# Inverse softmax sums turned by TensorE transposes instead of a trip through DRAM, with new delays for the instruction streams

## The chip, the core and the metric

The kernel runs on one core of a Trainium2 chip. A core has a matrix engine (TensorE, PE in the profile), a vector engine (VectorE, DVE), an engine for activation functions and copies (ScalarE, ACT), a general engine (GpSimd, POOL) and a queue that issues most of the transfers (SyncE, SP). Each takes its instructions in the order in which they were written for it, and waits on semaphores for the others. TensorE reads SBUF and writes PSUM, which has eight banks of 128 x 512 float32. The metric is the device time of one execution in microseconds (us); lower is better.

## What is computed

One decoder layer on 512 tokens of width 1024, in float32. One projection of the normed input feeds eight heads of block attention (512 columns each for q, k, v) and eight heads of a gated delta rule (`gdn`, chunks of 64 tokens, with a triangular solve per chunk and a scan over the chunks). Both outputs go through one output projection, then comes an MLP with squared ReLU. With two blocks of 256 tokens and up to three selected, the attention here comes down to causal attention with a relative bias:

```python
h = rms_norm(x, pre_mix_norm[l])
proj = jnp.einsum('bsd,dc->bsc', h, w_in[l])
...
o_att = moba_attention(q, k, v, rel_bias)      # softmax(q k / 8 + bias[distance]) v
o_gdn = gated_deltanet(gdn_qkv, gdn_z, gdn_a, gdn_b, conv_w[l], A_log[l], dt_bias[l], gdn_norm_w[l])
mix = jnp.einsum('bsc,cd->bsd', jnp.concatenate([o_att, o_gdn], axis=-1), w_out[l])
x = x + rms_norm(mix, post_mix_norm[l])
h = rms_norm(x, pre_mlp_norm[l])
m = jnp.einsum('bsf,fd->bsd', jnp.square(jax.nn.relu(jnp.einsum('bsd,df->bsf', h, w_up[l]))), w_down[l])
x = x + rms_norm(m, post_mlp_norm[l])
```

The change touches the division by the sum of the softmax, which the kernel does as a product with the inverse sum after P V.

## The kernel before

**Stages.** First the input is scaled and the first four columns of the projection are built (`head`). Then the other columns of the projection run (`projections`, `by_token`), and beside them the attention and the preparation of the delta rule. Every product that must be exact is split: a float32 operand is cut in a high and a low part of a faster format, and three matmuls (`mm3`) stand for one. The attention goes by four pairs of heads, p = 0 to 3. `scores` makes, for a pair, four rows of blocks (q = 3, 2, 1, 0, of 512, 384, 256 and 128 keys): six matmuls from `pt` into PSUM tag `a`, the bias and the row minimum on DVE (L688), and the exponential with its row sum on ACT (L690). Then DVE inverts the sums (L693). `values` turns the blocks of P by TensorE transposes (k = 3 to 0, helper line L103), copies them to SBUF tiles `ph` on ACT (L718), multiplies them by V and, on DVE, multiplies the product by the inverse sums (L738).

**The way of the sums before.** The sums lie with the query on the partition (128 x 4 x 2), but the product P V has the query along the free axis. So the inverse sums are written to DRAM (`d_s`, L694, 1024 single floats) and read back twice, each time spread over 64 partitions (L697), into `R8`. All three transfers are issued by SP, and the two reads wait for the write.

**What sets the order.** PE's order is written out by hand: a small planner (`Weave`) runs the streams (`scores`, `values`, `chunks`, `inverse`, `scan`, `finish_o`, `projections` and others) against a clock of its own that only counts matmul time. A stream gives a delay (`WAIT`, for the n-th use `SINGLE`) or a mark on which it waits, and the one of lowest `RANK` that is due goes next. The other engines' instructions are placed by a scheduler, with `LEAD` as extra urgency for a stream.

**The stages that the prediction speaks of.** `inverse` solves the triangles on DVE, `scan` starts by merging the halves (PE products of 32 x 32, `UT` and `uap` read back from DRAM by L774 and L771), then multiplies `UT` by `kB`, then makes eight steps: PE, a copy `vn` on ACT (L854), PE, DVE. `finish_o` norms the scan's output, and four transposes (`ot`) and the gate `zs` give `mg`. The projection's weights come through two buffers `w_raw` (SP L151), are cut by ACT into `w_hi` (L156) and by DVE or POOL into `w_lo` (L157). The weights of the output projection (`wo_raw`, L143, ACT L144, DVE L145) use the same two buffers at first. After the scan, the rest of the projection's columns and the last pair, PE has only the output projection to do, which starts with `ps_mm<-wo_h,mg_h`. From there to the end one product follows the other.

Of the kernel before, what the change touches and what calls it, by code (L numbers as in the profile page):

```python
# [11 lines left out]
FT = mybir.dt.float32  # L12
# [75 lines left out]
def layer(ctx, tc, nc, x, x_t, x_t0, w_first, w_in, w_v, w_ab, w_out, w_up, w_down, conv_w, a_log, dt_bias, gdn_norm_w, rel_bias,  # L88
# [13 lines left out]
    def transpose(o, i, k=128):  # L102
        nc.tensor.transpose(o, i, ident[:k, :k])  # L103
        weave.now += k * 4 / 2400
# [9 lines left out]
    dram = pool("dram", space=DRAM)  # L114
# [5 lines left out]
    at = pool("att", 2, stack=sA)  # L120
# [56 lines left out]
    def bank(tag="g", shape=(128, 512)):  # L177
        return psum.tile(list(shape), FT, name="ps_" + tag, tag=tag, bufs={"mm": 2, "g": 3, "a": 3}[tag])
# [281 lines left out]
    rkb, egc, gc, gl = (by5[:, i] for i in (1, 3, 4, 5))  # L460
# [198 lines left out]
    rows_of, sums_of = {}, {}  # L659


    def scores():
        for p in range(4):
            yield f"a{p}"
            if p:
                yield f"turned{p - 1}"
            T = [pts[p][:, i] for i in range(4)]
            Es = []
            for hh in range(2):
                E = at.tile([128, 512], FT, name="E")  # L670
                nc.sync.dma_start(E, bass.AP(tensor=d_e.tensor, offset=d_e.offset + 640 * (2 * p + hh), ap=[[1, 128], [1, 512]]))
                Es.append(E)
            Ls = [at.tile([128, 1280], FT, name="L") for _ in range(2)]
            mins = at.tile([128, 4, 2], FT, name="mins")
            sums = at.tile([128, 4, 2], FT, name="sums")
            for q in (3, 2, 1, 0):
                w = 128 * q + 128
                qs = slice(128 * q, 128 * q + 128)
                s = [bank("a") for _ in range(2)]
                for n, (i, j) in enumerate(((0, 2), (0, 3), (1, 2))):  # L680
                    for hh in range(2):
                        hs = slice(64 * hh, 64 * hh + 64)
                        mm(s[hh][:, :w], T[i][hs, qs], T[j][hs, :w], start=n == 0, stop=n == 2)
                weave.now -= 3 * w / 2400
                for hh in range(2):
                    l = Ls[hh][:, 64 * q * (q + 1):64 * q * (q + 1) + w]
                    rows_of[p, hh, q] = l
                    nc.vector.tensor_tensor_reduce(out=l, in0=s[hh][:, :w], in1=Es[hh][:, w - 1::-1], scale=1.0, scalar=3e38,  # L688
                                                   op0=OP.add, op1=OP.min, accum_out=mins[:, q, hh:hh + 1])
# [4 lines left out]
            nc.sync.dma_start(d_s[p].rearrange("q h t -> t q h"), sums)  # L694
            sums_of[p] = at.tile([128, 512], FT, name="R8", bufs=1)
            for hh in range(2):
                nc.sync.dma_start(sums_of[p][64 * hh:64 * hh + 64].rearrange("p (q t) -> p q t", q=4), d_s[p, :, hh].partition_broadcast(64))  # L697
# [4 lines left out]
    def values():  # L702
        for p in range(4):
# [319 lines left out]
    up = lambda g, k: w_up[2 * g:2 * g + 2, k // 4, :, k % 4].rearrange("a p n -> p a n")  # L1023
# [212 lines left out]
    t1, t2 = both[:, :, Z[0]], both[:, :, Z[1]]  # L1236
# [104 lines left out]
    rs = {}  # L1341
# [171 lines left out]
```

## Time and profile before

| what | value |
|---|---|
| median of 3 runs | 659.45 us (654.26 to 661.19) |
| the profiled execution | 654.6 us, its span 652.8 us |
| VectorE, ScalarE, GpSimd busy | 463.9, 354.7, 139.9 us |
| mean clock granted to TensorE | 0.969 |
| bytes moved by DMA | 114.53 MB |

The span is the time from the first to the last instruction of the profiled execution. A line of the timeline gives the start, the duration of the group, engine, line, operation, what it writes and reads, how many instructions, and in brackets how long the engine had been idle and what released it. Matmuls overlap, so the next row's start says more than a row's duration. A line of windows gives a stretch, its length, the busy time of the five engines with the number of instructions, the clock granted to TensorE (1.00 is full), the share of the DMA engines and GB/s.

### The profile page before, as it was taken

Reading aid. Unit: us, or ns where it says so; the run is one execution under the profiler, and the core shown is the slowest. Engines: PE = TensorE matmul, PEld = TensorE weight load, DVE = VectorE, ACT = ScalarE, POOL = GpSimd, SP = SyncE. Lnnn points to the kernel's source line nnn. Section 1 sums busy time; section 2 is a strip of 40 time slices with the busy share of each in tenths; the row PEclk is TensorE's granted clock in tenths of the full one; section 3 lists DMA queues with packets and bytes.
Section 4 is the critical chain, followed back from the end, with each engine's and each line's share of the span. In section 5 each row is a group of like instructions: output and inputs, shape, how many; then the busy total and the mean of one; then the engine's idle time right before and its main releaser. Section 6 shows DMA issues by size and latency. Waiting matters only on the chain.

```text
span 652.8 us, 10879 instructions
## 1 busy us (share of the span) xinstructions
PE 623.8 (96%) x4225; PEld 527.2 (81%) x4225; DVE 463.9 (71%) x673; ACT 354.7 (54%) x598; POOL 139.9 (21%) x176
## 2 busy tenths in 40 slices
PE   9989999999979989499999999999999999999995
PEld 7767777878747778378899899999998888888884
DVE  6688773999505455276564678888779888888876
ACT  8378573353726436244441576566566656655661
POOL 1435636101112232101412112211111230000001
PEclk9999999999959979789999999999999999999999
DMA  9332324323831203393378989999989999967603
GB/s 315 97 91 65 103 77 119 97 77 92 176 43 43 57 33 84 67 306 110 130 265 259 219 217 256 221 257 285 256 234 345 328 293 290 281 193 293 217 1 129
DMA packets 67635, 114.53 MB, mean 175 GB/s; under 512 B 20088, under 2 KB 41720, under 8 KB 67200
## 3 DMA queue, kind: packets, MB, share of 16 engines
q1 hardware_dynamic: 49888, 84.48, 39.7%
q0 software_dynamic: 17696, 29.36, 21.6%
q8 instruction: 33, 0.54, 0.4%
q14 instruction: 18, 0.15, 0.1%
HBM read 108.02 MB, written 35.17 MB: 219 GB/s over the span
## 4 chain that ended last, share of the span: by engine, by line
PE 83%; DMA 7%; DVE 5%; ACT 2%; issue 2%; SPq 1%; POOL 1%; POOLq 0%; DVEq 0%; ACTq 0%
PE ps_mm L99 38%; PE ps_g L99 26%; PE ps_a L99 16%; DMA d_s<-sums 3%; DMA w_raw<-in_w_in 1%; DMA wo_raw<-in_w_out 1%; PE ps_a L103 1%; DVE conv L383 1%; PE ps_g L103 1%; DMA UT<-d_u 1%; ACT w_hi L156 0%; SPq L774 0%; POOL w_lo L157 0%; SPq L697 0%; DVE pt L133 0%
## 5 line engine op out<-in xcount | busy, mean ns | idle before, releaser
L132 ACT CAST wdh<-wd 128x1024 fp32r<-128x1024 f32 x53 | 55.9, 1054 | 51.4 <-PE ps_mm L99 22.6
L133 DVE TENSOR_TENSOR u_l<-w,u_h 128x1024 fp32r<-128x1024 f32 x46 | 56.2, 1224 | 37.2 <-ACT u_h L132 35.5
L133 DVE TENSOR_TENSOR wdl<-wd,wdh 128x1024 fp32r<-128x1024 f32 x53 | 64.9, 1224 | 22.2 <-ACT wdh L132 22.1
L132 ACT CAST u_h<-w 128x1024 fp32r<-128x1024 f32 x46 | 47.9, 1046 | 56.7 <-PE ps_a L99 20.3
L99 PE MATMUL ps_mm<-hT_h,w_hi 128*128 128x512 f32 x168 | 71.1, 423 | 0.0
L99 PE MATMUL ps_mm<-hT_h,w_lo 128*128 128x512 f32 x168 | 66.3, 395 | 0.0
L99 PE MATMUL ps_mm<-hT_l,w_hi 128*128 128x512 f32 x168 | 66.3, 395 | 0.0
L1183 POOL DMA_DIRECT2D d_T<-in_w_down x32 | 33.0, 1031 | 143.3 <-DMA d_T<-in_w_down 85.7
L156 ACT CAST w_hi<-w_raw 128x512 fp32r<-128x512 f32 x50 | 30.9, 619 | 52.8 <-PE ps_mm L99 15.1
L157 POOL TENSOR_TENSOR w_lo<-w_raw,w_hi 128x512 fp32r<-128x512 f32 x26 | 33.5, 1287 | 55.3 <-ACT w_hi L156 46.9
L99 PE MATMUL ps_mm<-wdh,u_h 128*128 128x512 f32 x116 | 45.3, 390 | 0.0
L99 PE MATMUL ps_mm<-wdl,u_h 128*128 128x512 f32 x116 | 45.2, 389 | 0.0
L99 PE MATMUL ps_mm<-wdh,u_l 128*128 128x512 f32 x116 | 45.1, 389 | 0.0
L99 PEld LDWEIGHTS ps_mm<-hT_h,w_hi 128*128 128x128 f32 x168 | 32.0, 191 | 10.3 <-issue 3.1
L99 PEld LDWEIGHTS ps_mm<-hT_h,w_lo 128*128 128x128 f32 x168 | 32.0, 190 | 7.2
L99 PEld LDWEIGHTS ps_mm<-hT_l,w_hi 128*128 128x128 f32 x168 | 32.1, 191 | 5.1
L133 DVE TENSOR_TENSOR u_l<-f,u_h 128x1024 fp32r<-128x1024 f32 x28 | 34.1, 1217 | 0.0
L99 PE MATMUL ps_g<-wdl,u_h 128*128 128x512 f32 x80 | 31.1, 389 | 0.0
L99 PE MATMUL ps_g<-wdh,u_l 128*128 128x512 f32 x80 | 31.1, 389 | 0.0
L99 PE MATMUL ps_g<-wdh,u_h 128*128 128x512 f32 x80 | 31.1, 389 | 0.0
L132 ACT CAST u_h<-f 128x1024 fp32r<-128x1024 f32 x28 | 29.3, 1045 | 0.0
L383 DVE SCALAR_TENSOR_TENSOR conv<-ps_mm,cw,conv 128x511 f32<-128x511 f32 (+2 forms) x33 | 24.5, 743 | 2.8 <-ACT conv L380 2.3
(469 smaller groups left out, 1816.5 us busy)
## 6 DMA issues: line engine op xcount, KB each, us to landing
d_T<-in_w_down POOLq DMA_DIRECT2D x48, 512.0 KB, 11.3
wd<-d_T SPq DMA_DIRECT2D x32, 512.0 KB, 6.2
w<-in_w_up SPq DMA_DIRECT2D x28, 512.0 KB, 8.7
wd<-in_w_down SPq DMA_DIRECT2D x24, 512.0 KB, 6.8
w_raw<-in_w_in SPq DMA_DIRECT2D x40, 256.0 KB, 2.6
wo_raw<-in_w_out SPq DMA_DIRECT2D x16, 256.0 KB, 3.8
d_T<-d_T POOLq DMA_DIRECT2D x8, 512.0 KB, 11.5
ww<-in_w_first SPq DMA_DIRECT2D x8, 256.0 KB, 5.3
```

The source lines that it names most:

```text
L99: nc.tensor.matmul(o, l, r, **kw)
L103: nc.tensor.transpose(o, i, ident[:k, :k])
L132: nc.scalar.copy(hi, src)
L133: tt(lo, src, f32(hi), op=OP.subtract)
L156: nc.scalar.copy(hi, raw)
L157: (sub or tt)(lo, raw, f32(hi), op=OP.subtract)
L383: stt(c[:, s:], p[:, :512 - s], cw[:, ft, j:j + 1], c[:, s:], op0=OP.mult, op1=OP.add)
L1183: nc.gpsimd.dma_start(d_T[t][k], block(b, second)[k], accum_op=OP.add, max_dma_last_dim=1024)
```

## The change

The inverse sums no longer go through DRAM. ACT copies them wide: `R8[query, (q, head, 64)]` holds each sum 64 times. In `values`, four transposes turn the four 128 x 128 parts of it into a PSUM bank of tag `a`, ACT copies that bank into a tile `t2`, and the product on DVE reads this tile. Per pair one write and two reads by SP go away, and two ACT copies and four transposes are added. The transposes stand in `values`, ahead of P V on PE.

Beside this all tables of the planner have new values: in `WAIT` and `SINGLE` most entries stay near their value, some change much (`sums` 14.4 to 3.22, `pv0` 0.63 to 2.84, `o` 2.71 to 4.85, `normed` 32.04 to 23.02).

```diff
-RANK = {'chunks': 4, 'inverse': 1, 'scan': 1, 'scores': 2, 'values': 2, 'finish_o': 4, 'take': 4}
-LEAD = {'chunks': 100, 'inverse': 0, 'scan': 0, 'scores': 0, 'values': 100, 'finish_o': 300, 'take': 50, 'take_a': 0}
+RANK = {'chunks': 2, 'inverse': 1, 'scan': 1, 'scores': 4, 'values': 5, 'finish_o': 2, 'take': 3}
+LEAD = {'chunks': 100, 'inverse': 200, 'scan': 0, 'scores': 0, 'values': 300, 'finish_o': 50, 'take': 50, 'take_a': 0}
...
-START = (13.17, 4.85, 20.5, 14.78, 32.12, 17.27)
-ORDER = "k0 q0 x0 y0 k1 q2 q1 k2 k3 z0 q3 x1 w0 v1 v0 v2 v3 y1 x2 y2 x3 y3 z2 z1 z3"
-LO_DVE = (22, 46)
+START = (12.84, 4.21, 21.48, 14.78, 31.92, 16.12)
+ORDER = "k0 q0 x0 y0 k1 q2 q1 k2 k3 z0 q3 x1 w0 v2 v1 v0 v3 y1 x2 y2 x3 y3 z2 z1 z3"
+LO_DVE = (22, 49)
...
-    d_s = dram.tile([4, 4, 2, 128], FT, name="d_s")
...
             nc.vector.reciprocal(sums, sums)
-            nc.sync.dma_start(d_s[p].rearrange("q h t -> t q h"), sums)
             sums_of[p] = at.tile([128, 512], FT, name="R8", bufs=1)
-            for hh in range(2):
-                nc.sync.dma_start(sums_of[p][64 * hh:64 * hh + 64].rearrange("p (q t) -> p q t", q=4), d_s[p, :, hh].partition_broadcast(64))
+            nc.scalar.copy(sums_of[p].rearrange("p (q h e) -> p q h e", q=4, h=2), sums[:, :, :, None].to_broadcast([128, 4, 2, 64]))
             mark(f"sums{p}", wait["sums"])
...
             yield f"sums{p}"
+            rs = bank("a")
+            for q in range(4):
+                transpose(rs[:, 128 * q:128 * q + 128], sums_of[p][:, 128 * q:128 * q + 128])
+            sums_of[p] = at.tile([128, 512], FT, name="t2")
+            nc.scalar.copy(sums_of[p], rs)
             yield wait["pv0"]
             po = bank("a")
```

What this does to the order at three places. First SP's queue from the end of the inverse to the weights of the output projection. Before (the names are those of the text; `x4` is a row of four in a line):

```order
L774 DMA UT<-d_u 32x32x32 x4
L671 DMA E<-d_e 128x512
L694 DMA d_s<-sums 128x8x1
L671 DMA E<-d_e 128x512
L151 DMA w_raw<-in_w_in 128x512 x2
L697 DMA R_1950<-d_s 64x4x128 x2
L151 DMA w_raw<-in_w_in 128x512
L671 DMA E<-d_e 128x512 x2
L694 DMA d_s<-sums 128x8x1
L697 DMA R_2429<-d_s 64x4x128 x2
L151 DMA w_raw<-in_w_in 128x512 x4
L143 DMA wo_raw<-in_w_out 128x512 x5
```

Now:

```order
L773 DMA uap<-d_t 32x16x32 x4
L151 DMA w_raw<-in_w_in 128x512 x2
L670 DMA E<-d_e 128x512 x2
L776 DMA UT<-d_u 32x32x32 x4
L151 DMA w_raw<-in_w_in 128x512
L670 DMA E<-d_e 128x512 x2
L151 DMA w_raw<-in_w_in 128x512 x5
L143 DMA wo_raw<-in_w_out 128x512 x16
```

No transfer of the sums is left in the queue, the weights of the output projection follow in one row of sixteen, and the four loads of `UT` moved behind one more `w_raw` load and both loads of the biases `E` of the third pair.

Second PE at the merge of the scan. Before:

```order
L103 MATMUL ps_a<-ident,L 128x128 x4
L99 MATMUL ps_g<-uap,NT 32x32 x64
L103 MATMUL ps_a<-ident,L 128x128 x6
L99 MATMUL ps_g<-UT,uap 32x32 x64
L103 MATMUL ps_a<-ident,L 128x128 x8
L99 MATMUL ps_g<-UT,kB 64x64 x16
L99 MATMUL ps_a<-ph,V 64x128 x2
L99 MATMUL ps_a<-ph,V 64x256 x2
L99 MATMUL ps_a<-ph,V 64x384 x2
L99 MATMUL ps_a<-ph,V 64x512 x2
L99 MATMUL ps_g<-UT,kB 64x64 x16
L99 MATMUL ps_a<-pt 128x512 x6
```

Now:

```order
L103 MATMUL ps_a<-ident,L 128x128 x10
L99 MATMUL ps_g<-uap,NT 32x32 x64
L103 MATMUL ps_a<-ident,L 128x128 x8
L99 MATMUL ps_g<-UT,uap 32x32 x64
L99 MATMUL ps_a<-pt 128x512 x6
L103 MATMUL ps_a<-ident,R_1947 128x128 x4
L99 MATMUL ps_g<-UT,kB 64x64 x16
L99 MATMUL ps_a<-pt 128x384 x6
L99 MATMUL ps_g<-UT,kB 64x64 x16
L99 MATMUL ps_a<-ph,V 64x128 x2
L99 MATMUL ps_a<-ph,V 64x256 x2
L99 MATMUL ps_a<-ph,V 64x384 x2
```

The transposes of P moved ahead of the two merges (`uap,NT` and `UT,uap`), and the third pair's scores (`pt`) and the new transposes of the sums (`R_1947`) stand between the merge and the products with `kB`.

Third PE's last rows ahead of the output projection, behind the last products of the projection. Before:

```order
L103 MATMUL ps_g<-ident,ot 128x128 x4
L103 MATMUL ps_a<-ident,L 128x128 x8
L103 MATMUL ps_g<-ident,ot 128x128 x8
L99 MATMUL ps_a<-ph,V 64x128 x2
L99 MATMUL ps_a<-ph,V 64x256 x2
L99 MATMUL ps_a<-ph,V 64x384 x2
L99 MATMUL ps_a<-ph,V 64x512 x2
L103 MATMUL ps_g<-ident,ot 128x128 x4
```

Now:

```order
L103 MATMUL ps_a<-ident,L 128x128 x8
L103 MATMUL ps_g<-ident,ot 128x128 x12
L103 MATMUL ps_a<-ident,R_2898 128x128 x4
L99 MATMUL ps_a<-ph,V 64x128 x2
L99 MATMUL ps_a<-ph,V 64x256 x2
L99 MATMUL ps_a<-ph,V 64x384 x2
L99 MATMUL ps_a<-ph,V 64x512 x2
L103 MATMUL ps_g<-ident,ot 128x128 x4
```

The four transposes of the sums (`R_2898`) now stand ahead of the last P V, and the transposes of the scan's output moved behind those of P. Between the last step of the scan and these rows PE had nine `mm3` of the projection before (six, then three behind six transposes of P) and has eleven now (six and five).

More of the change, by code (lines that the diff above doesn't have):

```diff
@@ L18 @@
 EPS = 1e-6
-WAIT = {'conv_k': 7.33, 'k': 5.9, 'conv_q': 3.64, 'q': 1.36, 'conv_v': 5.51, 'v': 7.41, 'z': 2.13, 'ab': 12.9, 'g': 15.77, 'scalars': 7.14, 'r_in': 0.59, 'r_out': 12.59, 'kk': 3.93, 'kk_out': 90.01, 'gl': 14.07, 'qk': 0.26, 'va': 2.24, 'a': 6.82, 'row': 2.31, 'rows': 3.08, 'pv': 1.79, 'att': 2.27, 'inverse': 3.84, 'merge': 5.84, 'p1': 3.73, 'p2': 2.68, 'w': 1.0, 'vn': 1.0, 'state': 2.77, 'o_in': 9.58, 'o': 2.71, 'wo': 6.02, 'wo_out': 19.59, 'normed3': 15.84, 'normed': 32.04, 'n': 7.46, 'up': 0.42, 'sums': 14.4, 'turned': 3.53, 'pv0': 0.63, 'bias': 1.73, 'h': 0.87}
@@ L24 @@
-RANK = {'chunks': 4, 'inverse': 1, 'scan': 1, 'scores': 2, 'values': 2, 'finish_o': 4, 'take': 4}
-LEAD = {'chunks': 100, 'inverse': 0, 'scan': 0, 'scores': 0, 'values': 100, 'finish_o': 300, 'take': 50, 'take_a': 0}
+WAIT = {'conv_k': 6.84, 'k': 4.78, 'conv_q': 7.22, 'q': 2.45, 'conv_v': 4.95, 'v': 10.28, 'z': 1.15, 'ab': 14.84, 'g': 13.43, 'scalars': 7.4, 'r_in': 2.82, 'r_out': 13.78, 'kk': 3.96, 'kk_out': 98.49, 'gl': 11.46, 'qk': 0.22, 'va': 2.24, 'a': 6.82, 'row': 2.51, 'rows': 2.98, 'pv': 2.64, 'att': 2.94, 'inverse': 3.84, 'merge': 7.07, 'p1': 4.28, 'p2': 1.54, 'w': 0.73, 'vn': 1.0, 'state': 2.77, 'o_in': 12.7, 'o': 4.85, 'wo': 5.51, 'wo_out': 15.2, 'normed3': 14.27, 'normed': 23.02, 'n': 6.91, 'up': 0.05, 'sums': 3.22, 'turned': 3.22, 'pv0': 2.84, 'bias': 1.62, 'h': 1.2}
@@ new lines @@
+SINGLE = {('inverse', 6): 2.02, ('row', 5): 0.98, ('inverse', 25): 0.05, ('pv', 2): 0.1, ('normed', 0): 10.87, ('wo', 1): 0.05, ('conv_q', 0): 14.72, ('inverse', 16): 0.05, ('row', 6): 0.4, ('vn', 1): 0.65, ('pv', 4): 2.77, ('inverse', 0): 0.64, ('pv', 6): 2.0, ('rows', 4): 2.24, ('conv_v', 0): 15.61, ('kk_out', 0): 0.67, ('inverse', 27): 0.23, ('row', 12): 1.98, ('state', 0): 0.18, ('vn', 4): 0.05, ('row', 9): 5.09, ('inverse', 20): 1.76, ('state', 4): 0.65, ('inverse', 28): 1.88, ('rows', 7): 8.36, ('kk', 0): 0.05, ('normed3', 0): 7.71, ('state', 5): 2.94, ('r_in', 3): 1.7, ('w', 3): 2.25, ('scalars', 0): 0.21, ('rows', 5): 4.88, ('row', 3): 1.74, ('ab', 0): 0.05, ('inverse', 12): 1.5, ('o_in', 0): 0.05, ('rows', 11): 7.28, ('row', 13): 3.19, ('row', 15): 2.64, ('row', 1): 2.67, ('r_out', 2): 3.58, ('rows', 8): 2.26, ('conv_k', 3): 5.25, ('normed', 1): 13.13, ('inverse', 2): 1.64, ('k', 1): 6.97, ('vn', 3): 0.05, ('q', 0): 4.49, ('inverse', 19): 1.66, ('inverse', 24): 0.74, ('wo', 11): 4.8, ('row', 10): 2.37, ('conv_k', 0): 7.83, ('normed', 2): 12.17, ('row', 2): 2.64, ('wo', 12): 3.14, ('r_in', 1): 0.05, ('up', 3): 0.05, ('wo', 4): 3.04, ('inverse', 4): 0.32, ('h', 1): 2.19, ('row', 14): 2.53, ('inverse', 1): 0.91, ('wo', 5): 8.75, ('r_out', 3): 4.24, ('inverse', 13): 0.97, ('h', 2): 1.08, ('conv_q', 2): 5.47, ('a', 2): 2.77, ('r_out', 0): 3.9, ('row', 7): 1.12, ('up', 7): 0.79, ('wo', 8): 8.51, ('inverse', 23): 0.15, ('inverse', 15): 0.93, ('q', 1): 5.57, ('inverse', 11): 0.05, ('rows', 15): 5.79, ('rows', 14): 4.74, ('inverse', 26): 0.05, ('inverse', 22): 0.05, ('rows', 3): 5.73, ('wo', 3): 7.58, ('merge', 0): 11.11, ('conv_v', 3): 11.68, ('p1', 0): 1.31, ('conv_v', 1): 9.98, ('k', 0): 6.53, ('inverse', 18): 0.56, ('inverse', 29): 0.05, ('wo', 13): 8.89, ('kk', 2): 2.32, ('a', 1): 4.28, ('wo', 10): 7.64, ('kk', 3): 4.12, ('wo', 7): 9.5, ('vn', 5): 1.18, ('inverse', 9): 0.05, ('vn', 2): 1.65, ('conv_k', 1): 6.29, ('inverse', 30): 0.05, ('wo', 15): 3.26, ('inverse', 7): 3.17, ('conv_q', 3): 5.06, ('conv_k', 2): 5.79, ('va', 0): 7.69, ('state', 1): 2.53, ('r_out', 1): 6.72, ('g', 0): 15.31, ('z', 3): 0.31, ('rows', 13): 1.37, ('o_in', 3): 16.03, ('rows', 2): 4.88, ('conv_v', 2): 11.06, ('a', 0): 7.62, ('r_in', 0): 0.05, ('rows', 0): 5.25, ('z', 2): 0.53, ('p2', 0): 1.08, ('wo', 0): 6.48, ('state', 3): 2.3, ('r_in', 2): 0.13, ('w', 0): 0.05, ('row', 0): 1.86, ('v', 1): 9.22, ('k', 2): 6.26, ('conv_q', 1): 3.93, ('o', 3): 0.05, ('up', 6): 0.05, ('row', 4): 2.42, ('rows', 1): 1.85, ('vn', 6): 0.96, ('z', 0): 1.84, ('turned', 3): 4.05, ('o', 2): 2.45, ('att', 0): 0.22, ('pv0', 2): 1.72, ('gl', 0): 10.95, ('up', 1): 0.05, ('o', 1): 5.04, ('v', 0): 7.58, ('up', 4): 0.05, ('sums', 1): 0.15, ('turned', 1): 2.4, ('sums', 2): 0.78, ('up', 2): 0.05, ('att', 1): 2.53, ('wo', 14): 8.35, ('att', 3): 0.12, ('o_in', 1): 10.24, ('up', 5): 0.18, ('w', 1): 0.34, ('o', 0): 5.72, ('wo', 2): 6.25, ('n', 1): 7.01, ('sums', 0): 3.63, ('pv0', 1): 2.44, ('row', 11): 0.85, ('bias', 0): 2.15, ('v', 2): 7.09, ('pv0', 3): 1.41, ('sums', 3): 3.77, ('up', 0): 0.05}
```

1 line of the change is left out of this document (removed).

## The prediction

> **What bounds the kernel now.** The page of the profile comes first: the span, the busy times, the chain that ended last by line.
>
> ```profile
> span 652.8 us, 10879 instructions
> PE 623.8 (96%) x4225; PEld 527.2 (81%) x4225; DVE 463.9 (71%) x673; ACT 354.7 (54%) x598; POOL 139.9 (21%) x176
> PE ps_mm L99 38%; PE ps_g L99 26%; PE ps_a L99 16%; DMA d_s<-sums 3%; DMA w_raw<-in_w_in 1%; DMA wo_raw<-in_w_out 1%; PE ps_a L103 1%; DVE conv L383 1%; PE ps_g L103 1%; DMA UT<-d_u 1%; ACT w_hi L156 0%; SPq L774 0%; POOL w_lo L157 0%; SPq L697 0%; DVE pt L133 0%
> core 0: 652.8 us, clock 0.969
> ```
>
> PE is busy for 623.8 of 652.8 us. The time is PE's work, plus 29.0 us in which it is idle, plus what a lower clock costs: by the mean clock of 0.969 in the last line, 623.8 x 0.031 = 19 us. The transfer that the change removes is the first of those on the chain, with 3% (about 20 us). Next, the waits of SP's queue say how long the trip holds it, and its timeline says where: the start, then the duration, of the transfers around it.
>
> ```profile
> SPq L151 <- POOL w_lo L157: 50.2, 16, 12.1
> SPq L697 <- DMA d_s<-sums: 37.2, 4, 10.1
> 56.79 0.37 SPq L694 DMA_DIRECT2D d_s<-sums  x1
> 67.28 1.32 SPq L697 DMA_DIRECT2D R<-d_s  x2
> 184.75 1.25 SPq L697 DMA_DIRECT2D R<-d_s  x2
> 210.61 0.37 SPq L694 DMA_DIRECT2D d_s<-sums  x1
> 221.00 1.41 SPq L697 DMA_DIRECT2D R<-d_s  x2
> 222.46 18.06 SPq L151 DMA_DIRECT2D w_raw<-in_w_in  x4
> 258.23 0.43 SPq L694 DMA_DIRECT2D d_s<-sums  x1
> 259.88 0.33 SPq L143 DMA_DIRECT2D wo_raw<-in_w_out  x1
> 269.81 1.25 SPq L697 DMA_DIRECT2D R<-d_s  x2
> 271.15 10.48 SPq L143 DMA_DIRECT2D wo_raw<-in_w_out  x10
> ```
>
> Four times the reads wait for the write of 1024 single floats, 37.2 us in all, and what stands behind them waits too. That is the queue's loss, not PE's. What PE loses shows in the windows of the stretches around the four blocks (the second column is PE's busy time, the number ahead of the DMA share is the clock):
>
> ```profile
> 68.00:84.00 16.00, 15.78 (x104) 12.36 (x102) 11.60 (x19) 8.32 (x19) 11.86 (x16) 1.00 0.41 117
> 176.00:196.00 20.00, 14.43 (x224) 9.91 (x222) 1.28 (x2) 6.88 (x14) 2.90 (x3) 0.57 0.50 61
> 228.00:240.00 12.00, 9.09 (x112) 7.88 (x113) 5.07 (x10) 3.05 (x6) 3.34 (x5) 0.72 0.07 23
> 255.86:279.64 23.78, 15.45 (x75) 10.31 (x74) 9.30 (x16) 9.52 (x20) 2.61 (x4) 0.81 0.42 82
> ```
>
> Idle time and clock together, a stretch loses its length less busy x clock. Behind the first pair's block (56.79 to 67.28) it is 16.00 - 15.78 = 0.2 us: that trip is hidden by the projection, and removing it pays nothing. In the other three it is 20.00 - 14.43 x 0.57 = 11.8, 12.00 - 9.09 x 0.72 = 5.5 and 23.78 - 15.45 x 0.81 = 11.3 us. These three decide the case, and whether the trip causes them has to be seen for each.
>
> **Third pair's trip (210 to 221).** The rows of ACT and PE that follow it:
>
> ```profile
> 225.68 0.62 ACT L156 CAST w_hi<-w_raw 128x512 fp32r<-128x512 f32 x1 [3.68 <-DMA w_raw<-in_w_in]
> 230.28 0.57 ACT L854 COPY vn<-ps_g 64x512 f32<-64x512 f32 x1
> 230.91 0.37 PE L99 MATMUL ps_g<-vn,kdec 64*64 64x64 f32 x2 [3.16 <-ACT vn L854]
> ```
>
> The load of `w_raw` is issued at 222.46, right behind the reads, and ACT stands 3.68 us for it; the scan's `vn` comes later than PE needs it, PE waits 3.16 us, and the clock falls to 0.72 over the stretch. Without the trip the load goes up to 10 us earlier. The bounds are 5.5 gained (the whole loss) and 0 (if `vn` is late by the scan's own chain PE, ACT, PE, DVE). I take 4.4: nearer the whole, since only the wait of 3.68 on this load is seen ahead of the late copy, less 1.1 for that chain.
>
> **Fourth pair's trip (258 to 270).** PE and ACT at the end of the scan, and the landing times of `wo_raw`:
>
> ```profile
> 272.54 2.83 PE L99 MATMUL ps_a<-ph,V 128*64 128x128 f32 x12 [6.41 <-ACT ph L718]
> 276.48 2.46 PE L99 MATMUL ps_a<-ph,V 128*64 128x512 f32 x4 [1.11 <-ACT ph L718]
> 279.64 0.78 PE L99 MATMUL ps_mm<-wo_h,mg_h 128*128 128x512 f32 x1
> 271.50 0.62 ACT L144 CAST wo_h<-wo_raw 128x512 fp32r<-128x512 f32 x1 [6.94 <-DMA wo_raw<-in_w_out]
> 272.02 0.47 ACT L718 COPY ph<-ps_a 128x384 f32<-128x384 f32 x1
> DMA to landing us min/median/max: 2.7/3.8/11.6
> ```
>
> The `wo_raw` issued at 259.88, into the write of the sums, takes 11.6 us to land where 2.7 is the least. ACT waits 6.94 us for it, and the copy `ph` stands behind that cast in ACT's order; PE waits 6.41 us for `ph`, then does the last P V at a low clock, in 2.83 + 2.46 = 5.3 us. The prices for what PE has to do there:
>
> ```profile
> 123.84 2.73 PE ps_mm L99 x12
> 131.84 2.87 PE L103 MATMUL ps_a<-ident,L 128*128 128x128 f32 x20
> 135.33 2.37 PE L99 MATMUL ps_a<-ph,V 128*64 128x128 f32 x16
> 183.78 1.97 PE L103 MATMUL ps_a<-ident,L 128*128 128x128 f32 x8
> 45.72 0.58 ACT L411 COPY kdec<-ps_g 128x512 f32<-128x512 f32 x1
> ```
>
> So an `mm3` is 2.73 / 4 = 0.68, a transpose 2.87 / 20 = 0.14 (at the low clock 1.97 / 8 = 0.25), a P V of 16 matmuls 2.37. From the end of the scan to the output projection PE has nine `mm3` (6.1), thirty transposes (4.3) and P V (2.4), 12.8 us at full clock in 23.78: 11.0 lost, as the window says. After, with the trip gone, the chain through ACT goes by the loads: two buffers, 2.7 landing and some 1.3 for cast and low part (0.62 on ACT, the like on DVE), 4.0 us per two loads. The `wo_raw` after the one of 271.50 (in the new order the last two copies `ph` stand behind that cast) then comes some 6 us after 259.88, by 266; PE reaches this P V after eleven `mm3` (7.5) and twenty-four of its transposes (3.4) ahead of it, at 266.8. About even, so I leave 1 us of wait and take 10.0 gained. Bounds: 11.0, and 4.0 if one such wait of 6.41 stays in another place and only the rest goes. The two `mm3` that moved here are neither gain nor loss: they are taken from an earlier place, of equal price while PE is busy there. The new order of the `ot` transposes costs nothing where PE waits for none of them: they stand behind the copies of P, with eleven `mm3` as their cover; if that cover failed, DVE's norm of `ot` would be late next.
>
> **Second pair's trip and the merge (174 to 196).** The reads go at 184.75, but no late load of weights follows them: the loss lies in the merge itself, small products that wait for `UT`.
>
> ```profile
> 170.80 0.29 DVE L688 CUSTOM_DVE_ANT_0 L<-ps_a,E 128x128 f32<-128x128 f32 x1
> 172.66 4.15 DMA UT<-d_u
> 176.95 0.88 PE L99 MATMUL ps_g<-UT,uap 32*32 32x32 f32 x45 [0.56 <-DMA UT<-d_u]
> ```
>
> The trip pays nothing here, and the order is worse. `UT` moves behind `w_raw` and both loads of `E`, whose buffers come free with the second pair's last product with `E`, at 171.09. The four issues of `UT` reach the last one at 172.66; behind two more issues on this queue, they end up to 3 us later, and `UT` lands near 179.7, not 176.81 (172.66 + 4.15). PE's wait of 0.56 becomes some 3.0: +2.4. Against it, the scores and the transposes of the sums now stand between the merge and `kB`, work that fills holes (it was done elsewhere). I take +1. Bounds: -4 (a third of the 11.8 filled) and +6 (a wait of 3 and, at the half clock that rules here, as much again).
>
> **The new work.** Sixteen transposes by 0.14 are +2.3 (1.9 if they fall in holes of PE for a fifth; 4.0 by the row at the low clock). Eight wide copies of ACT by 0.58 (the copy of 128 x 512 from PSUM is the nearest row) are 4.6 us, beside PE: ACT is busy 54%. The last copy, of the turned sums, and the product on DVE are a chain of which only the P V of 2.4 us covers 0.58; should ACT be held by a cast, up to 1 us shows, and the range has it. The first wide copy stands early in ACT's order and costs nothing. The trip's twelve transfers leave SP, and by the new `LO_DVE` three low parts go from POOL to DVE: POOL at 21% loses nothing; DVE at 71% gains some 2 us of work, beside PE. The other delays move work without adding any: 0, between -2 and +3 (the hole of 3.16 as the size of one new wait). Everything from the output projection on stands in the same order on PE: 0.
>
> **A rule against it.** The row of twenty transposes, at 131.84, ran at 0.14 each, and the P V behind it at full speed:
>
> ```profile
> 133.00:135.00 2.00, 1.87 (x13) 1.63 (x14) 2.00 (x5) 2.00 (x6) 0.00 (x0) 1.00 0.36 123
> ```
>
> The clock in it is 1.00. The Trainium skill, page "TensorE: Matmul & The Clock Gate", section "Part 4: PE-mode transpose", says that the full clock doesn't engage for transposes, which don't count as work of TensorE in the same way. By that rule the long rows of transposes that the change makes would slow the matmuls behind them; this row speaks against it, at least for 2.9 us in a row.
>
> **The sum.** -10.0 (fourth pair) - 4.4 (third) + 1 (merge) + 2.3 (transposes) = -11.1. The profiled execution took 654.6, so 643.5. The three runs' median is 659.45, 4.85 above it; I carry half, as a stall's length differs from run to run and the stalls are what goes: 643.5 + 2.4 = 646.
>
> **The rivals.** First, the tail's wait moves. Sixteen loads of `wo_raw` stand in a row, and the cast ahead of the last `ph` has to wait for its own; if the buffers come free late, the 6.94 us come back for the 1 that I left, and P V at half clock costs 5.3 - 2.4 = 2.9 more: +8.8, so about 655. For it: ACT's order still puts the copies behind casts. Against: only the two loads of this stretch ever met the write of 1024 floats.
>
> Second, the other side: `UT`. SP's queue goes in order, and the longest wait of `w_raw` for POOL's low part was 12.1 us; if such a wait stands ahead of `UT`, the merge's PE is idle so long, and the 20 us of it at half clock cost 20.00 x (1 - 0.57) = 8.6: +20.7 in place of +1, about 646 + 19.7 = 666, slower than before by 1%. It decides from a wait of some 8 us on, where with the clock it eats the 14.4 of the two gains. In a mild form (5 us) it gives 651. For it: `w_raw` stands ahead of `UT` now. Against: low parts were on time there before.
>
> Third, the clock in transposes: twenty-four in a row at the tail (8 of P, 12 of `ot`, 4 of the sums; 3.4 us). If such a row lowers the clock, it costs 24 x (0.25 - 0.14) = 2.6, and P V behind it 2.9 more: +5.5, 651. The row at 133 speaks against. That is what the rule of the Trainium skill above comes to.
>
> Fourth, the change doesn't do what it says: the holes belong to the scan's chain and come back under other names, and only the new work is left: 654.6 + 2.3 + 2.4 = 659.
>
> **How the numbers follow.** Forecast 646: 0.60, its own range 639 to 651 (the bounds of the third pair's and the merge's terms). Tail 655: 0.14. `UT` mild 651: 0.10, and as a slower kernel 666: 0.04. Transposes' clock 651: 0.08. No effect 659: 0.04. The range reaches from 637 (all of 5.5 and 11.0, and 4 of the merge) to 656, which takes in the tail. About 1% is what a measurement of this kernel can tell from no change, so faster means under 652.9 and slower over 666.0. Under 652.9 lie the forecast, the mild case, the clock's case and a little of the tail: 0.60 + 0.10 + 0.08 + 0.05 = 0.83; between, 0.13; above, 0.04.
>
> **What would show it.** Right: no transfers of sums, `wo_raw` landing in under 5 us, no wait of PE for `ph` of over 2 us, and 255.86 to 279.64 shorter by about 10, with a clock near 1.00; no wait of ACT of 3.68 ahead of `vn`, and the scan's steps with a clock over 0.9. Wrong on the merge: `UT` waits of over 3 us on PE. Wrong on the rule: a clock under 1.00 right behind the row of transposes while PE waits for nothing. The whole is wrong if PE's idle time falls by less than 8 of 29.0 us, or if new idle time shows in the stages where the tables moved work.

## The result, and the profile after

The changed kernel takes 629.7 us (median of 4 runs, 628.8 to 631.5) where the kernel before takes 657.6 in the same comparison: the ratio is 0.958, with a 95% interval of 0.952 to 0.964. Forecast were 646 and a range of 637 to 656: faster, but by 4.2% and not by 2%. First the changed kernel's page (span, busy times) and its clock:

```profile
span 627.6 us, 10899 instructions
PE 613.9 (98%) x4241; PEld 521.9 (83%) x4241; DVE 463.8 (74%) x676; ACT 358.2 (57%) x606; POOL 136.8 (22%) x173
core 0: 627.6 us, clock 0.994
```

PE is idle for 13.7 us instead of 29.0, and the clock is 0.994 instead of 0.969. Where it went shows in windows. The changed kernel runs its later stages earlier, so from the scan on a stretch has to be matched by its work and not by its time: the scan runs from 200 to 255.86 before and to 240.75 after, and the output projection starts at 279.64 before and at 255.10 after. These are the kernel before in two stretches that the prediction did not show, and then the changed kernel in the stretches of the same stages:

```profile
28.00:72.00 44.00, 40.18 (x234) 28.82 (x233) 37.26 (x75) 29.99 (x80) 20.24 (x25) 0.96 0.28 85
200.00:255.86 55.86, 52.70 (x634) 42.82 (x632) 29.08 (x72) 29.86 (x65) 13.00 (x17) 0.94 0.18 53
```

```profile
28.00:72.00 44.00, 41.37 (x263) 29.64 (x265) 38.92 (x77) 32.73 (x84) 21.83 (x26) 1.00 0.26 81
176.00:196.00 20.00, 18.18 (x372) 13.94 (x374) 5.48 (x19) 12.25 (x31) 6.63 (x6) 0.83 0.07 19
200.00:240.75 40.75, 40.56 (x462) 32.59 (x457) 25.74 (x59) 22.43 (x47) 8.48 (x13) 1.00 0.15 48
240.75:255.10 14.35, 13.91 (x85) 10.82 (x83) 8.59 (x15) 9.38 (x19) 2.94 (x4) 1.00 0.36 125
```

Length less busy x clock, before and after:

| stretch | lost before, us | lost after, us | gained |
|---|---|---|---|
| 28 to 72 | 44 - 40.18 x 0.96 = 5.4 | 2.6 | 2.8 |
| 176 to 196 (merge) | 11.8 | 20 - 18.18 x 0.83 = 4.9 | 6.9 |
| 200 to the end of the scan (third pair) | 55.86 - 52.70 x 0.94 = 6.3 | 40.75 - 40.56 = 0.2 | 6.1 |
| end of the scan to output projection (fourth pair) | 11.3 | 14.35 - 13.91 = 0.4 | 10.9 |

26.7 us together, less 2.3 for the new transposes, against 25.2 us of span. The first row can't be put down to the change: other kernels below without single floats lose between 2.7 and 7.1 us in that stretch. The third and fourth pair went as forecast, to the ends of their bounds. The surprise is the merge: +1 was forecast, 6.9 were gained. In the trace of before, PE's timeline of that stage has a releaser that the prediction passed over:

```profile
178.28 1.61 PE L99 MATMUL ps_g<-UT,uap 32*32 32x32 f32 x60 [0.45 <-issue]
182.03 0.42 PE L99 MATMUL ps_g<-UT,uap 32*32 32x32 f32 x7 [2.14 <-issue]
183.27 0.58 PE L99 MATMUL ps_g<-UT,uap 32*32 32x32 f32 x14 [0.81 <-issue]
189.89 4.10 PE L99 MATMUL ps_a<-ph,V 128*64 128x256 f32 x10 [1.61 <-issue]
180.00:182.00 2.00, 0.00 (x0) 0.12 (x1) 0.00 (x0) 0.04 (x1) 0.00 (x0) 0.50 0.51 32
```

PE waits four times, 5.0 us in all, for nothing that the profile names. The last row is a window in the middle of it: hardly any engine works, the DMA engines are half busy, and move 32 GB/s. It lies between 174.29, when the single floats of the second pair were sent off, and 184.75, when the reads could start. What the DMA engines have in that window, how long the two loads of `w_raw` take that SP issued right behind the write (from 175.35 on), and, for comparison, a window of the first pair's trip in which the write is alone in flight (61 to 67):

```profile
DMA packets 34, 0.06 MB, mean 32 GB/s; under 512 B 3, under 2 KB 3, under 8 KB 34
q1 hardware_dynamic: 34, 0.06, 50.8%
DMA to landing us min/median/max: 12.4/12.4/12.4
DMA packets 0, 0.00 MB, mean 0 GB/s; under 512 B 0, under 2 KB 0, under 8 KB 0
```

So the busy DMA engines are not seen at the floats themselves. Of the 34 packets 31 have the size of a row of the loads issued behind the write (2 KB), and each takes 0.48 us on average (0.508 x 16 engines x 2 us / 34). A write alone in flight shows no packet for most of its 10 us, though it isn't complete. The changed kernel has no wait named issue on PE at all; the wait for `UT` grew, as was forecast, from 0.56 to 2.02 us, with the clock low for some 7 us behind it:

```profile
177.81 2.58 PE L99 MATMUL ps_g<-UT,uap 32*32 32x32 f32 x126 [2.02 <-DMA UT<-d_u]
179.00:186.00 7.00, 7.00 (x137) 5.28 (x132) 1.95 (x7) 4.50 (x10) 1.73 (x2) 0.52 0.02 6
```

So there are two theories, and a third by the change's other half. T: the write of 1024 single floats slows, for its 10 us, whatever is in flight beside it, PE's instructions too. F, the forecast's: what costs is SP's queue standing behind the write. O: the merge's gain comes from the new order.

### The profile page after: what moved, and what is told of

It is laid out like the page before. It is cut to its first block, busy times and chain, and to the rows that moved or that the text cites. A ratio compares the mean times of both kernels' runs of the same rounds, so it can differ in the third digit from the quotient of the medians.

```text
span 627.6 us, 10899 instructions
## 1 busy us (share of the span) xinstructions
PE 613.9 (98%) x4241; PEld 521.9 (83%) x4241; DVE 463.8 (74%) x676; ACT 358.2 (57%) x606; POOL 136.8 (22%) x173
## 4 chain that ended last, share of the span: by engine, by line
PE 88%; DMA 4%; DVE 3%; ACT 2%; SPq 1%; issue 1%; POOL 1%; POOLq 0%; DVEq 0%; ACTq 0%
PE ps_mm L99 43%; PE ps_g L99 26%; PE ps_a L99 16%; DMA ww<-in_w_first 2%; PE ps_a L103 2%; PE ps_g L103 1%; DMA wo_raw<-in_w_out 1%; DVE conv L383 1%; DMA UT<-d_u 1%; DMA cload<-in_c_sel 1%; SPq L776 0%; ACT L L689 0%; ACT wo_h L144 0%; DMA abw<-in_w_ab 0%; POOL UT L768 0%
## 5 line engine op out<-in xcount | busy, mean ns | idle before, releaser
L133 DVE TENSOR_TENSOR u_l<-w,u_h 128x1024 fp32r<-128x1024 f32 x46 | 56.2, 1224 | 37.2 <-ACT u_h L132 35.3
L157 POOL TENSOR_TENSOR w_lo<-w_raw,w_hi 128x512 fp32r<-128x512 f32 x23 | 29.8, 1297 | 36.3 <-ACT w_hi L156 28.2
L687 DVE CUSTOM_DVE_ANT_0 L<-ps_a,E 128x512 f32<-128x512 f32 (+3 forms) x32 | 14.4, 487 | 17.9 <-PE ps_a L99 17.8
```

Of the source, the lines that this page charges most:

```text
L133: tt(lo, src, f32(hi), op=OP.subtract)
L157: (sub or tt)(lo, raw, f32(hi), op=OP.subtract)
```

## Experiments

### The same trip with the floats in rows

The order of all engines stays that of before; only the write of the sums takes 128 rows of 32 bytes, not 1024 floats (for all pairs, or for one). The reads are the same.

```diff
-            nc.sync.dma_start(d_s[p].rearrange("q h t -> t q h"), sums)
+            nc.sync.dma_start(d_s[p].rearrange("q h t -> (q h t)").rearrange("(t e) -> t e", e=8), sums.rearrange("p q h -> p (q h)"))
```

> The kernel before with one thing changed: the 1024 inverse sums of a pair are written to DRAM as 128 rows of 8 floats, not as 1024 single floats; the order of every engine is that of before, and the two reads stay. The sums then lie in another order in DRAM, so the attention is divided by the wrong ones. Theory T (the write of single floats itself keeps the DMA engines so slow that loads beside it land late, and that PE's own instructions come late, the waits named issue at the merge): the trip shrinks from 10 us to under 4, the merge loses 6 less of its 11.8, the third pair 4 to 5.5 less, the fourth 10 to 11 less, the first about 2 less: 22 to 25 us under before. Rival F (the steps of the forecast: only queued loads are late, the merge's loss is not the trip's): 14.4 under before, the waits named issue stay. Rival O (the gain at the merge comes from the new order): as F at the merge.

> As the run with all pairs, for the second pair alone (the trip that starts at 174), so that only its sums are permuted. T: the four waits of PE named issue (5.0 us) go, and the low clock behind them is shorter: 5 to 8 us under before. F and O: within 1 us of before, the waits named issue stay.

> The same for the fourth pair alone (the trip that starts at 258). T and F: PE's wait of 6.41 for ph falls under 1.5, the clock stays near 1.00, 9 to 11 us under before. If the casts of wo_raw are late by the buffers and not by the write: under 5.

> The kernel before with the sums of the first pair alone written as 128 rows of 8 floats (so only its sums are permuted). F: 0, PE has the projection to do there. T: 0 to 3 us, for the short low clock at 60 to 68 in the profile before (4.00 x 0.24 + 3.47 x 0.18 = 1.6), if the write is what leads to it.

> The same for the third pair alone. F and T: PE's wait of 3.16 for vn goes and with it the low clock, 4 to 6 us under before. With the 8.0 and 8.3 measured for the second and the fourth pair and 23.0 for all four, the first and the third come to 6.7 together if the pairs add up.

| write in rows for | us | ratio to before, 95% interval | gained, us |
|---|---|---|---|
| all pairs | 633.6 | 0.963, 0.958 to 0.968 | 23.0 |
| first | 652.1 | 0.993, 0.990 to 0.996 | 4.7 |
| second | 648.6 | 0.985, 0.979 to 0.991 | 8.0 |
| third | 649.9 | 0.989, 0.986 to 0.993 | 7.0 |
| fourth | 648.3 | 0.987, 0.981 to 0.992 | 8.3 |

One instruction's pattern, with nothing moved, is worth 23 us, as T said and F did not. (In these kernels the inverse sums come back in another order; their instructions, sizes and places are those of before.) The single gains add to 28.0, more than 23.0; each has an interval of about 2 to 4 us to either side, so whether the pairs overlap stays open. In parts T's numbers were missed too: the first pair brings more than its 0 to 3, the third more than 4 to 6, the fourth less than 9 to 11, with a wait for `ph` of 1.9 left where under 1.5 was expected. Of the run with all pairs, the wait of SP's queue for the writes (four times, 9.2 us for 37.2), the longest wait of PE at the merge, and that window:

```profile
SPq L697 <- DMA d_s<-sums: 9.2, 4, 3.2
PE ps_g L99 <- issue: 1.7, 1, 1.7
176.00:196.00 20.00, 18.27 (x383) 13.88 (x376) 4.90 (x12) 11.83 (x26) 6.63 (x6) 0.83 0.32 75
```

The merge loses 20 - 18.27 x 0.83 = 4.8, as in the changed kernel, with the old order. O is out for the merge's main part. The wait named issue shrinks from 5.0 to 1.7 but does not go, against T's expectation (in the run of the second pair alone it is 2.5 + 0.2); what releases PE there stays open. The trips take 2.9 to 4.9 us, the longest being the second, not under 4 as expected.

The first pair had been put at 0. In the run of the second pair alone, whose order and first trip are those of before, PE has a wait at the projection that the profile of before doesn't have. SP's rows ahead of it, and the wait:

```profile
59.29 0.37 SPq L694 DMA_DIRECT2D d_s<-sums  x1
70.36 1.33 SPq L697 DMA_DIRECT2D R<-d_s  x2
71.79 11.43 SPq L151 DMA_DIRECT2D w_raw<-in_w_in  x5
81.33 0.63 PE L103 MATMUL ps_g<-ident,kraw 128*128 128x128 f32 x4 [2.90 <-DVE kraw L387]
```

The load of `w_raw` stands behind the reads, and the chain from it through the cast, the convolution and `kraw` ends too late by 2.90 us. The run of the fourth pair alone has the same wait with 2.12, though its load goes at 68.91, about as early as before's 68.71. What decides is which of the two comes first, DVE's `kraw` or PE. Counted from the issue of the write, `kraw` starts after 21.2 us in the run of the second pair alone, 20.4 in that of the fourth and 19.8 before; PE comes to it after 19.1, 19.1 and 20.6. In the profile of before PE was the later one, since it ran at half clock just ahead, and no wait shows:

```profile
62.50:66.00 3.50, 3.50 (x39) 2.97 (x36) 3.17 (x6) 1.60 (x6) 0.00 (x0) 0.51 0.00 0
```

That this hid the late load in the one execution that the prediction read is argued, not isolated. By length less busy x clock, the stretch from 54 to 84 loses 30 - 28.85 x 0.94 = 2.9 before, 4.7 in the run of the second pair alone and 3.2 in that of the fourth, and 0.8 to 1.3 in the runs whose first floats are not written singly. But the run of the third pair alone, which does write the first floats singly, loses 1.1 there and has no such wait. So the first trip costs in some runs and not in others. As the profiled run with the first pair in rows took 654.7, no less than that of before, no trace shows where all of the 4.7 lies.

### The write alone, beside the changed kernel

The changed kernel, with each pair's sums also written to DRAM, by nobody read and by nobody waited for; once as single floats, once as rows.

```diff
             nc.vector.reciprocal(sums, sums)
+            nc.sync.dma_start(d_s[p].rearrange("q h t -> t q h"), sums)
             sums_of[p] = at.tile([128, 512], FT, name="R8", bufs=1)
```

> The changed kernel, and beside it each pair's sums are still written to DRAM as 1024 single floats, which nobody reads or waits for; SP's queue waits for none of them. T (the write holds the DMA engines): waits of PE for UT or named issue come back at the merge, wo_raw and w_raw land 6 to 11 us late: 8 to 20 us over the changed kernel. F (what cost was the wait of SP's queue for the write): within 2 us of the changed kernel.

> The changed kernel with the unread writes of the sums as in the run with single floats, in the same place of every queue, but as 128 rows of 8 floats. T (the count of single floats in flight is what holds the DMA engines): within 3 us of the changed kernel, where the write of single floats cost 23. If any write of the sums there costs (its issue, its wait, its place ahead of UT): over 10.

Single floats: 652.7 us, 23 over the changed kernel (ratio to before 0.994, 0.991 to 0.998). Rows: 630.1 us, no difference to it (0.958, 0.955 to 0.961). SP waits for the completion of the write in neither, and the order is the same in both, so F falls: that wait is not what costs. The 23 are more than the 8 to 20 that T had. Single floats first: SP's rows at the merge, PE's longest waits for `UT`, and the landing times of `UT`; the last row is the landing of `UT` with the rows.

```profile
178.27 0.37 SPq L694 DMA_DIRECT2D d_s<-sums  x1
178.74 9.07 SPq L778 DMA_DIRECT2D UT<-d_u  x4
PE ps_g L99 <- DMA UT<-d_u: 9.2, 2, 7.8
DMA to landing us min/median/max: 10.6/11.5/11.6
```

```profile
DMA to landing us min/median/max: 4.3/4.4/4.9
```

Loads of `UT` that are issued right behind the write land after 11.5 us instead of 4.4, and even their issue takes 9.07 us (3.61 with the rows).

These loads, like those of `w_raw` and `wo_raw`, come from SP's own queue. By themselves they can't tell T from a queue that works its transfers off in order behind a slow one. The blocks of instructions of 16 KB come over another queue (`q8`). Here is the share of the sixteen DMA engines that one block took: some 8 us into the third pair's write in the kernel before (218 to 223), at the same place in the run where that pair's floats go in rows (217 to 222), and 3 us into the second pair's unread write (181 to 189):

```profile
q8 instruction: 1, 0.02, 4.3%
q8 instruction: 1, 0.02, 1.5%
q8 instruction: 1, 0.02, 4.2%
```

That is 0.043 x 16 x 5 = 3.4 us with single floats against 0.015 x 16 x 5 = 1.2 with rows, and 0.042 x 16 x 8 = 5.4 us beside the unread write. In the changed kernel the blocks up to 320 us take 0.9 to 1.5. So another queue is slowed too, as T says, if by fewer microseconds than SP's own; blocks at the very start of a write are not (1.3 to 1.6). A write of single floats issued by another engine's queue was not run, so how much is due to sharing SP's queue stays open, and so does why the write is so slow.

One part of T is not shown. In the kernel before three of PE's four waits named issue lie between 177 and 187, and there the profile lists packets of SP's queue and no instruction block:

```profile
DMA packets 839, 0.63 MB, mean 63 GB/s; under 512 B 532, under 2 KB 532, under 8 KB 839
q1 hardware_dynamic: 839, 0.63, 76.8%
```

That PE waited for its own instructions there is thus a guess. Shown is that the waits shrink or go with the single floats.

### One half of the change at a time

The transposes in the kernel before, with its old tables; and the new tables with the old trip. The diffs are the two halves of the change's own.

> The transposes of the sums in the kernel before, with all its tables (delays, ranks, leads, order of the columns) unchanged. T: 20 to 24 us under before, no wait of PE named issue at the merge, some 2 of it given back for the sixteen transposes; so close to the changed kernel, and the tables worth little (0 to 4 us). F: 11 to 12 under before. O: the merge keeps its loss of about 11, and the rest of the changed kernel's gain is owed to the tables.

> The changed kernel's tables with the old way of the sums through DRAM. T: the write of single floats now stands ahead of the loads of UT, so the merge loses at least as much as before, and the casts of wo_raw meet the fourth write again: 648 to 662 us, far from the changed kernel. O (the gain is the new order's): 630 to 642.

The transposes alone: 633.5 us (0.964, 0.959 to 0.968). The tables alone: 663.6 us, slower than before (1.011, 1.007 to 1.016). Both are as T said, the second just beyond its end; only a wait of PE named issue, of 1.3 us, is left at the merge of the first, where T had none and no sums are written at all. That merge loses 20 - 18.20 x 0.83 = 4.9, with the old order: once more the order is not what counts. The transposes bring 23.1 us of the gain, as much as the rows do. The tables' 3.8 more beside them are not clear of noise (the intervals of 0.959 to 0.968 and 0.952 to 0.964 overlap); with the trip the tables cost 7. With the trip they put `UT`'s loads behind the single floats, which is what the run with the unread write shows by itself.

### Twice the transposes

```diff
-            for q in range(4):
+            for q in (0, 1, 2, 3, 0, 1, 2, 3):
```

> The changed kernel with each of the sixteen transposes of the sums made twice, into the same place. T: +2.3 us (16 by 0.14), the clock behind them unchanged. The rival of the clock in transposes: +5 or more, with P V of the fourth pair at half clock behind 28 transposes in a row.

635.2 us, 5.5 over the changed kernel: by its sum nearer to the rival's. But the place decides. PE ahead of the last P V, and the window of it:

```profile
253.11 1.47 PE L103 MATMUL ps_g<-ident,ot 128*128 128x128 f32 x12
254.41 1.04 PE L103 MATMUL ps_a<-ident,L 128*128 128x128 f32 x8
255.29 1.04 PE L103 MATMUL ps_a<-ident,R 128*128 128x128 f32 x8
257.77 2.37 PE L99 MATMUL ps_a<-ph,V 128*64 128x128 f32 x16 [1.45 <-ACT ph L715]
253.00:256.00 3.00, 3.00 (x29) 2.91 (x28) 2.43 (x4) 2.22 (x5) 0.00 (x0) 1.00 0.40 142
```

Twenty-eight transposes in a row take 3.2 us at a clock of 1.00, and P V behind them its full-speed 2.37. The rule that the Trainium skill gives (page "TensorE: Matmul & The Clock Gate", section "Part 4: PE-mode transpose") does not slow this row. What is over 2.3 us lies elsewhere: PE waits 1.45 for `ph` here (0.44 in the changed kernel), and the merge loses 20 - 17.11 x 0.74 = 7.3 instead of 4.9: PE waits longer for `UT` (0.90 + 1.84), and the eight transposes and small products behind that wait run at the low clock that starts there. So the rival is refuted for rows of up to 3.2 us; longer rows were not run.

### The hole that is left

The changed kernel's 2.02 us for `UT`, filled and then removed. First by order: one delay longer, so that scores and transposes stand ahead of the merge's second products.

```diff
-('p1', 0): 1.31
+('p1', 0): 5.0
```

> The changed kernel with one delay longer (the first use of p1, 1.31 to 5.0), so that the first scores of the third pair and the four transposes of the sums stand ahead of the merge's second products, which wait 2.02 us for UT, and not behind them. If PE's idle time there starts the low clock of the 7 us behind it: the wait falls under 0.8 and the low clock goes or is short, 2 to 5 us under the changed kernel. If the scores or the later order only move the hole: within 1 us.

636.7 us, 7 over the changed kernel, which neither side expected: PE no longer waits for `UT`, but the later order shifts with it, and new waits come: for `ph` (1.8) ahead of the last P V, and at the start of the output projection (for `mg_l` 1.1 and 0.7, for `om` 0.7). The low clock of the merge did not go either, since PE now waits 1.5 for `kB`: the stretch loses 20 - 17.79 x 0.83 = 5.2. The hole was moved, not filled.

Then by what `UT` waits for. In the changed kernel's chain its loads follow POOL's memset of the whole tile, though only two quarters have to be zero.

```diff
-        nc.gpsimd.memset(UT, 0.0)
+        for b in (1, 3):
+            nc.gpsimd.memset(UT[32 * b:32 * b + 32, :, :, 0:32], 0.0)
```

> The changed kernel with only those two quarters of UT set to zero that nothing else writes, so that the loads of UT need not wait for the memset on POOL; they then stand ahead of the biases E in SP's queue. If UT is late by memset and queue: PE's wait of 2.02 goes, and with it most of the low clock behind it (176 to 196 lost 4.9): 2 to 5 us under the changed kernel. If UT is late by its own landing (4.25) or the scan is late by other work: within 1 us.

627.6 us (0.955, 0.952 to 0.957), the lowest median of all, some 2 under the changed kernel, which is at the edge of the noise (0.952 to 0.964 there). Its window of the merge:

```profile
176.00:196.00 20.00, 18.64 (x437) 14.52 (x431) 6.62 (x24) 15.46 (x37) 6.59 (x6) 1.00 0.21 65
PE ps_g L99 <- issue: 1.1, 1, 1.1
```

No wait for `UT`, a clock of 1.00, 1.4 us lost instead of 4.9; one wait named issue of 1.1 is back, beside the biases that now load at that time.

## Why the prediction was wrong

**The step that failed** is the second pair's: "The trip pays nothing here, and the order is worse", +1. Its trip was worth 8.0 us by itself, and without single floats the merge loses 4.8 to 4.9 us instead of 11.8, in the old order as in the new. The argument looked for a late load behind the reads, found none, and put the loss on small products that wait for `UT`. PE's timeline had another name: issue, 5.0 of some 5.6 us of idle time. And the landing times had the pointer: two loads of `w_raw` of 12.4 us, issued behind the write and ahead of the reads. The sign that the prediction gave for being wrong on the merge, a wait for `UT` of over 3 us, looked only for a worse merge, and did not come (2.02).

**In numbers:** by medians 13.5 us were forecast (659.45 to 646) and 27.9 measured. Of the 14.4 between, the single runs show 9.0 at the merge, 4.7 at the first pair, 2.6 at the third and -1.7 at the fourth; they add to more than the rows bring together, and the tables may have brought some. The range's low end is set out as "all of 5.5 and 11.0, and 4 of the merge"; these terms give 646 - 1.1 - 1.0 - 5.0 = 639, not 637. The measured time lies outside by either.

**Behind it** stands a model that was too narrow: a slow transfer as something that its own queue waits for. The unread write shows that it is a cost to transfers in flight beside it, waited for or not: loads of its own queue, and instruction blocks of another. The `wo_raw` of 11.6 us was quoted, and was the hint: it had been issued before any read stood in the queue. The Trainium skill, page "DMA: Bandwidth & Descriptors", section "Issuing engines are not separate DMA queues", says that transfers run on the same sixteen DMA engines and interleave, whichever engine started them. The 11.5 us of `UT` don't bear on that, being of the write's own queue; the instruction block of 5.4 us beside the write agrees.

**First pair, 0:** measured 4.7 (3 to 7 by its interval). The cover was read from one execution, in which PE came to `kraw` later than it, and from a window that starts at 68, behind the trip; the stretch from 54 to 84 loses 2.9 there. Two other executions with the same first trip wait 2.12 and 2.90 us for `kraw`, one does not.

**Third pair, 4.4:** 7.0 by itself (4.9 to 9.2 by its interval), 6.1 in the profile over the whole rest of the scan. The step was right, the size too careful: the scan loses 0.2 now, so its own chain left nothing of the wait.

**Fourth pair, 10.0:** 8.3 by itself (5.6 to 12 by its interval), 10.9 in the profile. Right, and the stage is 9.4 us shorter, though two `mm3` more stand in it.

**Merge's order, the +2.4 within the +1:** the wait was right by itself, 2.02 against 3.0 forecast. The low clock behind it, 7 us at 0.52, was only in the bound.

**New work, 2.3:** the transposes take 0.13 to 0.15 each and none is at half clock but those of the merge. The transposes alone gain as much as the rows, whose trip is left with 3 to 5 us, so no larger cost is seen. **Tables, 0 (between -2 and +3):** -3.8, beyond the bound but not clear of noise.

**The rivals.** The tail's wait did not move: PE waits 0.44 for `ph`, though `wo_raw` takes up to 6.5 us to land (median 3.3), over the 5 that the prediction gave as a sign. `UT` came late, mildly. The clock in transposes is refuted for rows of up to 3.2 us. That the change would not do what it says is out. What was missing is a rival on the faster side: that removing the write frees more than the queue.

## What to carry to other kernels

A transfer of very many tiny pieces is to be priced by what is in flight beside it, on its own queue above all and, as seen here, on the instruction queue, not only by who waits for its completion. Look for the landing times of what was issued right behind it, and for a window in which the DMA engines are busy and move little; the pattern of the transfer can be changed by itself to find out. And a stretch that looks covered in one execution is not free: it takes other executions, or a run without the transfer, to price it.

## What the runs showed of the hardware

- 1024 floats written singly, 4 KB in all, take 9 to 11.6 us, and what is issued behind them lands late: `UT` 11.5 us for 4.4, `w_raw` 12.4, `wo_raw` 11.6. The same bytes in 128 rows of 32 take 3 to 5 us from their issue to the reads, and delay nothing that could be measured (630.1 for 629.7 us).
- Instruction blocks of 16 KB took 1.8 to 6.9 us when they came 3 to 8 us into a write of single floats (3.4 to 3.9 at one place where rows left 1.2), and 0.9 to 1.5 us in the changed kernel.
- PE's waits named issue at the merge: 5.0 us beside single floats (DMA share 0.50), 1.7 beside rows (0.32), 1.3 and 1.1 in two kernels that write no sums at all (0.21 each), none in the changed kernel's quiet merge (0.07). The Trainium skill, page "Runtime: NRT & Kernel Launch", section "Instruction fetch mechanics", says that each engine fetches its instructions in blocks over a DMA queue of its own, a cost that it calls mostly hidden. That these waits are such fetches is not shown: no block moves between 177 and 187 in the kernel before, where three of its four waits lie.
- 2.02 us of waiting at the merge was followed by 7 us at a clock of 0.52 with PE fully busy; 1.1 us, in the last run, was followed by no low clock.
- Twenty-eight float32 transposes in a row, 3.2 us, ran at a clock of 1.00, and the matmuls behind them at full speed.
